# A shared expert's gate and up products moved next to the output projection, and its down product moved ahead of the routed experts

## Chip, cores and metric

The kernel runs on one core of a Trainium2 chip. The metric is the device time of one execution in microseconds, the median of several runs.

## What is computed

Two transformer blocks on 256 tokens of width 1024. The change lies in the second half of the first block, a mixture of 64 routed experts and one shared expert:

```python
x = x + g1 * (jnp.concatenate([y_fox, y_rwkv], axis=-1) @ w_out[l])
h = rms_norm(x, norm2_g[l]) * (1 + sc2) + sh2
x = x + g2 * moe_ffn(h, router_w[l], router_bias[l], exp_w_gate[l], exp_w_up[l], exp_w_down[l],
                     sh_w_gate[l], sh_w_up[l], sh_w_down[l])
# moe_ffn: each token takes 6 of 64 experts, with weights from the sigmoid scores
routed = routed_experts(hf, idx, wts.astype(h.dtype), w_gate, w_up, w_down)
shared = swiglu(hf, sw_gate, sw_up, sw_down)       # (silu(x @ wg) * (x @ wu)) @ wd, inner width 256
```

The norm multiplies each token by one factor r (from the mean square of its 1024 values) and each feature by a gain; then a shift per feature is added. So a product of h with a weight W is r times the product of (gain x) with W, plus the product of the shift with W, which is the same for all tokens.

## The kernel before

All activations are kept transposed, features on the 128 partitions and the 256 tokens (T) along the free axis, as 8 chunks of 128 features (NK). Matmul weights come through a ring of 1 MB buffers: `weights` takes the next buffer in turn and issues the load on SyncE's queue (SP), in program order; a load waits until its buffer's last user is done. The ring is put together in `phase_a`: 3 buffers (RING), 2 more (RINGX) and 7 more (RINGY) that take the place of earlier tiles when the mixers of the first block are finished. The kernel is written against a framework that tracks tiles, puts in all waits and fixes the order of the instructions of each engine when the program is built: earlier lines of the program go first where several are ready by its model, so a later line can be drawn forward into a pause.

Around the change the program runs like this.

- `phase_a` ends with `w_out(1)`, the second half of the output projection. It yields once for each of the 8 chunks d. Each step splits weights in two parts (ACT copies the high part `wh`, GpSimd, called POOL, subtracts the low part `wl`), runs 12 matmuls in PSUM, and DVE adds the residual into `xT[:, d]` (x1). Then `score(d)` multiplies the chunk with the router's weights and squares it (`ssum`, `rsq`).
- After the last chunk `router` forms the norm's factor y per token (`rms2`, `rsqrt`), the scores `lg`, and `rs2`, the factor laid out along the free axis, by a matmul with the diagonal `rdg`.
- `phase_b` calls `route` (a chain of small DVE operations: top groups, top 6, prefix counts by five small matmuls `ps<-rmb,rbef`), then forms the normalised input h2 (shown as `h`) in 8 chunks with DVE, ACT and POOL. `choose(0)` builds the selection matrix P of the first group and its weights (`rtab`, `ws`).
- h2 is transposed on PE (L1194) and split in a high part `hh` (ACT) and a low part `hl` (DVE).
- `shared` is a generator: its first step is the gate product `mm<-h,w` and Silu, before the loop; its second step, the up product, comes after group 0, its third, the down product `acc<-sT,w`, after group 1. h2 lies in one of the two buffers of the tag "xg" until up is done.
- The loop runs over 16 groups of 4 experts. `experts` gathers tokens (`ps<-P,hh` and `ps<-P,hl`, 32 matmuls in four PSUM tiles), evicts them to xg (L1469, DVE and ACT in turn), then for 8 weight units of gate/up and 4 of down multiplies 32 columns per expert (`mm<-w,xg`, `mm<-second,xg`, `mm<-w,hT`, `mm<-second,hT`); "second" is a copy of a unit's part for a second expert (L1484). The results are split (`yh` on ACT, `yl` on DVE) and scattered into four accumulators in PSUM (`acc<-PT,yh`, `acc<-PT,yl`). All 16 groups and the shared expert add into the same accumulators, and the first of them all clears them with `start`.

A product of plain f32 operands, as those of the shared expert, shows as two matmul instructions. All helpers have one line each: matmuls L318, tensor_tensor L325, tensor_scalar L328, scalar_tensor_tensor L331, activations L337, the ring's loads L293.

Of the kernel before, what the change touches and what calls it, by code (L numbers as in the profile page):

```python
# [25 lines left out]
NEG = -1e30  # L26
RING = 3
RINGX = 2
RINGY = 7
NF = 7  # L30
NE = 8
NG = 3
# [233 lines left out]
class Prog:  # L266
# [242 lines left out]
    def phase_a(self):  # L509
        nc = self.nc  # L510
        ctx = ExitStack()
        with ctx:
# [204 lines left out]
            self.xT = late.tile([128, NK, T], F32, name="xT")  # L717
            self.more("ringX", RINGX)
            self.late = ExitStack()
            score = self.router(self.pool("router", ctx=self.late, side="right"))  # L720
            self.more("ringY", RINGY, self.late)
            if self.dbg and "catT" in self.dbg:
                for i in range(4):
                    nc.sync.dma_start(self.dbg["catT"][:, 2 * i:2 * i + 2, :], cat[i])
            for d in w_out(1):
                self.stt(self.xT[:, d, :], self.o[d // 2][:, d % 2, :], self.mod[:, 16 + d:17 + d], x0[d // 2][:, d % 2, :],
                         OP.mult, OP.add)
                score(d)
            self.show("x1T", self.xT)

    def rwkv_prepare(self, big, low, proj, hf):
# [427 lines left out]
    def phase_b(self):  # L1159
        nc = self.nc  # L1160
        ctx = ExitStack()
        with ctx:
            self.psum, self.banks = self.pool("psumB", space=PSUM, ctx=ctx), {"mm": 2, "ps": 2}
            self.pacc = self.pool("pacc", space=PSUM, bufs=1, ctx=ctx)
            self.wk, self.nsq = self.pool("wkB", bufs=2, ctx=ctx), 2
            bb = self.pool("bigB", bufs=1, ctx=ctx)
            self.copied = [None, None]
            R = self.route(bb)

            rs, gs = self.rs2, self.gs2  # L1170

            def normed():
                h2 = self.wk.tile([128, NK, T], F32, tag="xg", name="h2")
                for k in range(NK):
                    self.stt(h2[:, k, :], self.xT[:, k, :], gs[:, k:k + 1], rs, OP.mult, OP.mult)
                    self.act(h2[:, k, :], h2[:, k, :], AF.Identity, bias=self.mod[:, 24 + k:25 + k])
                return h2
            h2 = self.wk.tile([128, NK, T], F32, tag="xg", name="h2")
            for k in range(NK):
                if k % 2:  # L1180
                    self.act(h2[:, k, :], self.xT[:, k, :], AF.Identity, scale=gs[:, k:k + 1])
                    self.tt(h2[:, k, :], h2[:, k, :], rs, OP.mult, nc.gpsimd)
                else:
                    self.stt(h2[:, k, :], self.xT[:, k, :], gs[:, k:k + 1], rs, OP.mult, OP.mult)
                self.act(h2[:, k, :], h2[:, k, :], AF.Identity, bias=self.mod[:, 24 + k:25 + k])
            self.show("h2T", h2)
            first = self.choose(0, R, bb)

            hh, hl = (bb.tile([128, 2, D], F32R, name=n) for n in ("hh", "hl"))
            for b in range(2):  # L1190
                for q in range(2):
                    ps = self.ps("mm")
                    for i in range(4):
                        nc.tensor.transpose(ps[:, 128 * i:128 * i + 128], h2[:, 4 * q + i, 128 * b:128 * b + 128],  # L1194
                                            self.ident)
                    o = slice(512 * q, 512 * q + 512)
                    nc.scalar.copy(hh[:, b, o], ps)
                    self.tt(hl[:, b, o], ps, hh[:, b, o].bitcast(F32), OP.subtract)
            acc = [self.pacc.tile([128, 2, T], F32, tag=f"acc{i}", name=f"acc{i}") for i in range(4)]
            shared = self.shared(h2, acc)  # L1200
            next(shared)
            for g in range(16):
                self.experts(g, R, first if g == 0 else self.choose(g, R, bb), hh, hl, acc)
                if g == 0:
                    self.unplaced(R, bb)
                next(shared, None)
            self.leftovers(R, normed, acc, bb)
            self.fewer(RINGY)
            for d in range(8):
                self.stt(self.xT[:, d, :], acc[d // 2][:, d % 2, :], self.mod[:, 40 + d:41 + d], self.xT[:, d, :],  # L1210
                         OP.mult, OP.add)
# [15 lines left out]
    def router(self, rt):  # L1227

        nc, rw, br = self.nc, self.rw, self.br
        self.lg = rt.tile([128, 2, 64], F32, name="lg")  # L1230
        self.act(self.lg[:, 0, 0:1], br[:, 0:1], AF.Sigmoid)
        self.rs2 = rt.tile([128, T], F32, name="rs2")
        s = rt.tile([128, T], F32, name="ssum")
        pl = self.ps()
        pm = self.ps()

        def score(k):
            for b in range(2):
                self.mm(pl[:, 64 * b:64 * b + 64], self.xT[:, k, 128 * b:128 * b + 128], rw[:, k, :], start=k == 0 and b == 0,
                        stop=k == NK - 1)  # L1240
            sq = s if k == 0 else rt.tile([128, T], F32, tag="rsq", name="rsq")
            self.act(sq, self.xT[:, k, :], AF.Square)
            if 0 < k < NK - 1:
                self.tt(s, s, sq, OP.add)
            if k < NK - 1:
                return
            for i, t in enumerate((s, sq)):
                for b in range(2):
                    self.mm(pm[:, b:b + 1], t[:, 128 * b:128 * b + 128], self.ones[:, 0:1], start=i == 0 and b == 0, stop=i == 1)
            x = rt.tile([128, 2], F32, name="rms2")  # L1250
            self.ts(x, pm[:, 0:2], 1.0 / D, EPS, OP.mult, OP.add)
            y = self.rsqrt(x)
            for b in range(2):
                self.stt(self.lg[:, b], pl[:, 64 * b:64 * b + 64], y[:, b:b + 1], br, OP.mult, OP.add)
            self.act(self.lg, self.lg, AF.Sigmoid)

            dg = rt.tile([128, T], F32, tag="rsq", name="rdg").rearrange("p (b t) -> p b t", b=2)
            for b in range(2):
                self.ts(dg[:, b], self.ident, y[:, b:b + 1], None, OP.mult)
                self.mm(pm[:, T + 128 * b:T + 128 * b + 128], self.ones, dg[:, b])  # L1260
            nc.scalar.copy(self.rs2, pm[:, T:])
        return score

    def shared(self, h2, acc):

        sT = self.wk.tile([128, 2, T], F32, tag="sq", name="sT", bufs=self.nsq)
        sg = self.wk.tile([128, 2, T], F32, tag="sq", name="sgs", bufs=self.nsq)
        for u in range(2):
            w = self.weights(self.a["sh_gu"][u]).rearrange("p (k n) -> p k n", k=NK)
            ps = self.ps("mm")  # L1270
            for c in range(2):
                o = ps[:, T * c:T * c + T]
                for k in range(NK):
                    self.mm(o, w[:, k, 128 * c:128 * c + 128], h2[:, k, :], start=k == 0, stop=k == NK - 1)
            for c in range(2):
                o = ps[:, T * c:T * c + T]
                if u == 0:
                    self.act(sg[:, c, :], o, AF.Silu)
                else:
                    self.tt(sT[:, c, :], sg[:, c, :], o, OP.mult)  # L1280
            yield
        w = self.weights(self.a["sh_d"], 2048).rearrange("p (f n) -> p f n", n=D)
        for d in range(8):
            for f in range(2):
                self.mm(acc[d // 2][:, d % 2, :], w[:, f, 128 * d:128 * d + 128], sT[:, f, :], start=False, stop=False)
        yield

    def route(self, bb):

# [162 lines left out]
    def experts(self, g, R, slots, hh, hl, acc):  # L1452
# [6 lines left out]
        for q in range(4):  # L1459
            ps = self.ps()  # L1460
            for i in range(2):
                d = 2 * q + i
                n = 0
                for b in range(2):
                    for part in (hh, hl):
                        self.mm(ps[:, T * i:T * i + T], part[:, b, 128 * d:128 * d + 128],
                                P[:, b].rearrange("p r s -> p (r s)"), start=n == 0, stop=n == 3)
                        n += 1
            (nc.scalar.copy if q % 2 else nc.vector.tensor_copy)(  # L1469
                xg[:, 2 * q:2 * q + 2, :].rearrange("p k t -> p (k t)"), ps)  # L1470
        eng = [nc.vector, nc.scalar, nc.vector, nc.scalar]
        reg = []
        for q in range(4):
# [32 lines left out]
        for n in range(2):  # L1506
# [7 lines left out]
            for r in range(2):  # L1514
# [5 lines left out]
                for i in range(4):  # L1520
                    d = 4 * n + i
                    for y in (yh, yl):
                        self.mm(acc[d // 2][:, d % 2, :], y[:, 128 * i:128 * i + 128], PT[:, r],
                                start=g == 0 and r == 0 and d % 2 == 0 and y is yh, stop=False)

    def leftovers(self, R, normed, acc, bb):

# [726 lines left out]
```

## Time and profile before

| | us |
|---|---|
| median of 3 runs | 1398.86 (1393.77 to 1401.87) |
| profiled execution | 1392.92 |
| its span, first to last instruction | 1390.9 |
| PE busy in the span | 1274.5 (92%) |
| DVE, ACT, POOL busy | 784.1, 656.0, 359.6 |

Engines: PE is TensorE's matmul row, PEld its weight loads, DVE VectorE, ACT ScalarE, POOL GpSimd, SP SyncE. A matmul's row is longer than the distance to the next one, since they overlap; for costs the distance of starts is read. The busy time of an engine is an average over stages with different limits, so the views below are taken stage by stage: the output projection is at 337 to 359 us, the expert loop at 384 to 900.

### The profile page before, as it was taken

Reading aid. Unit: us, or ns where it says so; the run is one execution under the profiler, and the core shown is the slowest. Engines: PE = TensorE matmul, PEld = TensorE weight load, DVE = VectorE, ACT = ScalarE, POOL = GpSimd, SP = SyncE. Lnnn points to the kernel's source line nnn. Section 1 sums busy time; section 2 is a strip of 40 time slices with the busy share of each in tenths; the row PEclk is TensorE's granted clock in tenths of the full one; section 3 lists DMA queues with packets and bytes.
Section 4 is the critical chain, followed back from the end, with each engine's and each line's share of the span. In section 5 each row is a group of like instructions: output and inputs, shape, how many; then the busy total and the mean of one; then the engine's idle time right before and its main releaser. Section 6 shows DMA issues by size and latency. Waiting matters only on the chain. (4 is left out here: it accounts for less than half of the span.)

```text
span 1390.9 us, 27073 instructions
## 1 busy us (share of the span) xinstructions
PE 1274.5 (92%) x10141; PEld 912.3 (66%) x10141; DVE 784.1 (56%) x2021; ACT 656.0 (47%) x1309; POOL 359.6 (26%) x310
## 2 busy tenths in 40 slices
PE   5888899999799999999999999979899877999996
PEld 4666777778645544444444444458788867999996
DVE  4679835555754355545555554468735457544444
ACT  2531323234364455555555555555444445455552
POOL 0133541103200000000000000044345731166662
PEclk9988999899799999999999999988899988999998
DMA  9443555124588899999999999742122433245530
GB/s 373 162 151 138 196 213 191 61 77 162 232 331 333 335 392 388 395 393 400 391 382 387 393 406 394 282 176 98 62 79 87 143 117 121 85 176 185 181 134 31
DMA packets 47080, 321.04 MB, mean 231 GB/s; under 512 B 5216, under 2 KB 5856, under 8 KB 9184
## 3 DMA queue, kind: packets, MB, share of 16 engines
q1 hardware_dynamic: 45072, 316.17, 58.3%
q10 hardware_dynamic: 1872, 3.08, 0.7%
q8 instruction: 82, 1.34, 0.4%
q14 instruction: 54, 0.44, 0.1%
HBM read 318.19 MB, written 1.05 MB: 230 GB/s over the span
## 5 line engine op out<-in xcount | busy, mean ns | idle before, releaser
L325 POOL TENSOR_TENSOR wl<-w,wh 128x512 fp32r<-128x512 f32 x221 | 290.4, 1331 | 373.1 <-ACT wh L310 247.9
L1484 ACT COPY second<-w 128x512 f32 x384 | 218.3, 619 | 103.9 <-PE mm L318 78.2
L318 PE MATMUL mm<-xh,wh 128*128 128x256 f32 (+1 forms) x768 | 230.5, 300 | 14.8 <-DMA w<-in_w_dram 4.7
L318 PE MATMUL mm<-xh,wl 128*128 128x256 f32 (+1 forms) x768 | 229.9, 300 | 4.0 <-POOL wl L325 3.4
L318 PE MATMUL mm<-xl,wh 128*128 128x256 f32 (+1 forms) x768 | 227.5, 296 | 0.2 <-DVE xl L331 0.2
L1484 DVE COPY second<-w 128x512 f32 x384 | 146.5, 427 | 103.0 <-PE mm L318 93.6
L310 ACT CAST wh<-w 128x512 fp32r<-128x512 f32 x196 | 119.6, 619 | 156.5 <-PE mm L318 117.8
L318 PEld LDWEIGHTS mm<-xh,wh 128*128 128x128 f32 (+1 forms) x768 | 155.6, 203 | 23.2 <-ACT xh L337 4.9
L318 PEld LDWEIGHTS mm<-xh,wl 128*128 128x128 f32 (+1 forms) x768 | 154.7, 202 | 9.6 <-POOL wl L325 4.8
L318 PEld LDWEIGHTS mm<-xl,wh 128*128 128x128 f32 (+1 forms) x768 | 155.2, 202 | 4.6 <-issue 2.1
L328 POOL TENSOR_SCALAR PT<-consts,ws 128x256 fp32r<-128x256 f32 x32 | 30.9, 978 | 474.3 <-DVE ws L1444 462.0
L318 PE MATMUL mm<-w,xg 128*32 128x512 f32 x1024 | 133.9, 594 | 0.0
L318 PE MATMUL mm<-second,xg 128*32 128x512 f32 x1024 | 133.5, 592 | 0.0
L318 PEld LDWEIGHTS mm<-second,xg 128*32 128x32 f32 x1024 | 34.3, 110 | 75.6 <-issue 68.0
L325 DVE TENSOR_TENSOR yl<-mm,yh 128x512 fp32r<-128x512 f32 x64 | 43.7, 689 | 62.1 <-ACT yh L1518 62.1
L318 PEld LDWEIGHTS mm<-w,xg 128*32 128x32 f32 x1024 | 32.0, 110 | 68.8 <-issue 63.1
L318 PE MATMUL mm<-second,hT 128*32 128x512 f32 x512 | 75.7, 594 | 0.0
L318 PE MATMUL mm<-w,hT 128*32 128x512 f32 x512 | 73.3, 602 | 2.5 <-ACT hT L1504 2.5
L318 PE MATMUL ps<-P,hh 128*128 128x256 f32 x256 | 67.6, 293 | 0.7 <-DVE xg L1469 0.7
L318 PE MATMUL ps<-P,hl 128*128 128x256 f32 x256 | 65.9, 287 | 0.0
L1518 ACT CAST yh<-mm 128x512 fp32r<-128x512 f32 x64 | 37.5, 585 | 52.2 <-PE mm L318 51.5
L318 PE MATMUL acc<-PT,yh 128*128 128x256 f32 x256 | 60.8, 287 | 0.3
(628 smaller groups left out, 2511.8 us busy)
## 6 DMA issues: line engine op xcount, KB each, us to landing
w<-in_exp_dram SPq DMA_DIRECT2D x192, 1024.0 KB, 9.4
w<-in_ada_dram SPq DMA_DIRECT2D x24, 1024.0 KB, 5.0
w<-in_ffi_dram SPq DMA_DIRECT2D x22, 1024.0 KB, 4.9
w<-in_w_dram SPq DMA_DIRECT2D x14, 1024.0 KB, 4.8
w<-in_w_in_dram SPq DMA_DIRECT2D x12, 1024.0 KB, 4.8
w<-in_ffo_dram SPq DMA_DIRECT2D x11, 1024.0 KB, 4.7
w<-in_w_out_dram SPq DMA_DIRECT2D x4, 1024.0 KB, 4.9
w<-in_mixout_dram SPq DMA_DIRECT2D x4, 1024.0 KB, 4.9
```

The costliest lines, as they stand in the source:

```text
L310: self.nc.scalar.copy(h, x)
L318: return self.nc.tensor.matmul(o, l, r, start=start, stop=stop, skip_group_check=True).ins
L325: (eng or self.nc.vector).tensor_tensor(out=o, in0=x, in1=y, op=op)
L328: (eng or self.nc.vector).tensor_scalar(out=o, in0=x, scalar1=s1, scalar2=s2, op0=op0, op1=op1)
L1484: c = (nc.scalar.copy if q % 2 else nc.vector.tensor_copy)(s[:, q:q + 1, :], w[:, bass.ds(reg[q], 1), :])
L1518: nc.scalar.copy(yh, ps)
```

## The change

- `gate_up` replaces the first two steps of `shared`. Ahead of the projection's second half it allocates `xg` (8 chunks of 256 columns and one more column), lets POOL copy the shift into that last column, and issues both loads of the shared expert. In each step d of the projection DVE writes gain times x1 into chunk d, without the norm's factor and without the shift. After the last step 64 matmul instructions of 257 columns form gate and up in four PSUM tiles; the last column is the shift's product. DVE copies that column (4 times), multiplies the rest by `rs2` (4 times) and, for up, adds and multiplies in one operation (2 times); ACT does Silu with the column as bias.
- The normalised h2 before the loop is gone. The transposes read `xg`; y, kept in `y2`, is put in where they are evicted: ACT's copy becomes an activation with a scale, DVE's subtraction a scalar_tensor_tensor.
- As the gathered rows now lack the shift, it is added in `experts` where gathers are evicted: on DVE an addition in place of a copy, on ACT two activations of 256 with a bias in place of a copy of 512.
- The down product stands ahead of the loop (`shared_down`), and clears the accumulators.
- RINGY is 6 instead of 7; `ssum` lies in another pool.

```diff
-RINGY = 7
+RINGY = 6
@@ phase_a
+            gu = self.gate_up()
             for d in w_out(1):
                 self.stt(self.xT[:, d, :], ...)
                 score(d)
+                self.ts(self.xg[:, d, :T], self.xT[:, d, :], self.gs2[:, d:d + 1], None, OP.mult)
+            gu()
@@ phase_b
-            h2 = self.wk.tile([128, NK, T], F32, tag="xg", name="h2")
-            for k in range(NK):
...
                     for i in range(4):
-                        nc.tensor.transpose(ps[:, 128 * i:128 * i + 128], h2[:, 4 * q + i, 128 * b:128 * b + 128],
+                        nc.tensor.transpose(ps[:, 128 * i:128 * i + 128], self.xg[:, 4 * q + i, 128 * b:128 * b + 128],
                                             self.ident)
-                    nc.scalar.copy(hh[:, b, o], ps)
-                    self.tt(hl[:, b, o], ps, hh[:, b, o].bitcast(F32), OP.subtract)
+                    self.act(hh[:, b, o], ps, AF.Identity, scale=y)
+                    self.stt(hl[:, b, o], ps, y, hh[:, b, o].bitcast(F32), OP.mult, OP.subtract)
-            shared = self.shared(h2, acc)
-            next(shared)
+            self.shared_down(acc)
             for g in range(16):
                 self.experts(g, R, first if g == 0 else self.choose(g, R, bb), hh, hl, acc)
-                next(shared, None)
+    def gate_up(self):
+        nc, rt = self.nc, self.rt
+        self.xg = xg = rt.tile([128, NK, T + 1], F32, name="xgain")
+        nc.gpsimd.tensor_copy(xg[:, :, T], self.mod[:, 24:32])
+        ws = [self.weights(self.a["sh_gu"][u]).rearrange("p (k n) -> p k n", k=NK) for u in range(2)]
+        def f():
+            self.sT = sT = rt.tile([128, 2, T], F32, name="sT")
+            sg = self.wk.tile([128, 2, T], F32, tag="sq", name="sgs", bufs=self.nsq)
+            for u in range(2):
+                for c in range(2):
+                    ps = self.ps(("po", "pt", "mm", "mm")[2 * u + c])
+                    for k in range(NK):
+                        self.mm(ps[:, :T + 1], ws[u][:, k, 128 * c:128 * c + 128], xg[:, k, :T + 1], start=k == 0, stop=k == NK - 1)
+                    t = (sT if u else sg)[:, c, :]
+                    b = self.wk.tile([128, 8], F32, tag="nx", name="gub", bufs=3)[:, :1]
+                    nc.vector.tensor_copy(b, ps[:, T:T + 1])
+                    self.tt(t, ps[:, :T], self.rs2, OP.mult)
+                    if u == 0:
+                        self.act(t, t, AF.Silu, bias=b)
+                    else:
+                        self.stt(t, t, b, sg[:, c, :], OP.add, OP.mult)
+        return f
@@ experts
-            (nc.scalar.copy if q % 2 else nc.vector.tensor_copy)(
-                xg[:, 2 * q:2 * q + 2, :].rearrange("p k t -> p (k t)"), ps)
+            p, sh = ps.rearrange("p (k t) -> p k t", k=2), self.mod[:, 24 + 2 * q:26 + 2 * q]
+            if q % 2:
+                for i in range(2):
+                    self.act(xg[:, 2 * q + i, :], p[:, i], AF.Identity, bias=sh[:, i:i + 1])
+            else:
+                self.tt(xg[:, 2 * q:2 * q + 2, :], p, sh[:, :, None].to_broadcast([128, 2, T]), OP.add)
```

## Rows read from the trace of the kernel before

**Rows 1.** Busy us by stretch: length, PE, PEld, DVE, ACT, POOL, clock, DMA.

```profile
337.00:359.00 22.00, 20.51 (x164) 19.45 (x162) 9.67 (x17) 9.99 (x20) 11.60 (x9) 0.99 1.00 418
359.00:384.00 25.00, 16.21 (x70) 12.71 (x71) 20.59 (x113) 8.98 (x20) 4.85 (x6) 0.66 0.32 132
...
630.00:662.00 32.00, 31.34 (x265) 14.61 (x264) 17.03 (x48) 18.19 (x34) 2.00 (x2) 1.00 0.99 396
```

**Rows 2.** Waits, 384 to 900 us: total us, times, longest; all engines, then SP's queue.

```profile
PEld mm L318 <- DMA w<-in_exp_dram: 4.7, 16, 0.3
...
SPq L293 <- PE mm L318: 322.3, 174, 28.9
```

**Rows 3.** PE's timeline in the loop: start us, length, instruction, how many merged.

```profile
389.22 1.06 PE L318 MATMUL mm<-w,xg 128*32 128x512 f32 x8
...
418.72 7.07 PE L318 MATMUL mm<-h,w 128*128 128x256 f32 x32
425.43 0.47 PE L318 MATMUL ps<-P,hh 128*128 128x256 f32 x1
...
429.34 1.06 PE L318 MATMUL mm<-w,xg 128*32 128x512 f32 x8
...
459.08 6.63 PE L318 MATMUL acc<-sT,w 128*128 128x256 f32 x30
...
468.72 1.07 PE L318 MATMUL mm<-w,xg 128*32 128x512 f32 x8
...
501.08 1.07 PE L318 MATMUL mm<-w,xg 128*32 128x512 f32 x8
...
629.96 1.06 PE L318 MATMUL mm<-w,xg 128*32 128x512 f32 x8
...
662.06 1.06 PE L318 MATMUL mm<-w,xg 128*32 128x512 f32 x8
```

**Rows 4.** PE ahead of the loop: timeline, then groups of 359 to 386 us.

```profile
358.59 0.28 PE L318 MATMUL fx<-yh,wl 128*128 128x256 f32 x1
...
384.18 0.47 PE L318 MATMUL ps<-P,hh 128*128 128x256 f32 x1
...
L318 PE MATMUL mm<-h,w 128*128 128x256 f32 x32 | 9.0, 443 | 1.0 <-issue 1.0
L1194 PE MATMUL mm<-consts,h 128*128 128x128 f32 x16 | 4.7, 438 | 5.1 <-ACT h L337 3.8 <-DVE hl L325 1.2
```

**Rows 5.** DVE, 359 to 384 us: groups (busy us, mean ns), then the timeline.

```profile
L331 DVE SCALAR_TENSOR_TENSOR h<-xT,gs,rs 128x256 f32<-128x256 f32 x4 | 2.8, 691 | 0.0
L325 DVE TENSOR_TENSOR hl<-mm,hh 128x512 fp32r<-128x512 f32 x4 | 2.7, 682 | 0.0
...
L331 DVE SCALAR_TENSOR_TENSOR xT<-fx,mod,x 128x256 f32<-128x256 f32 x1 | 0.5, 484 | 0.9 <-PE fx L318 0.9
...
379.32 0.68 DVE L325 TENSOR_TENSOR hl<-mm,hh 128x512 fp32r<-128x512 f32 x1
```

**Rows 6.** SP's timeline: loads issued from 330 us on.

```profile
335.34 0.33 SPq L293 DMA_DIRECT2D w<-in_sh_gu_dram  x1
337.04 47.86 SPq L293 DMA_DIRECT2D w<-in_exp_dram  x12
```

**Rows 7.** ACT and DVE evictions: groups of 500 to 890 us; timeline at 367 us.

```profile
L1469 ACT COPY xg<-ps 128x512 f32<-128x512 f32 x25 | 14.6, 585 | 36.5 <-PE ps L318 36.5
...
L1469 DVE COPY xg<-ps 128x512 f32<-128x512 f32 x25 | 17.3, 692 | 15.8 <-PE ps L318 15.8
...
366.98 1.31 ACT L337 ACTIVATE h<-h,mod 128x256 f32<-128x256 f32 x3 [0.18 <-POOL h L325]
```

**Rows 8.** Busy us in steps of 2 us, columns as in the first group.

```profile
358.00:360.00 2.00, 1.76 (x17) 1.68 (x15) 0.48 (x1) 0.42 (x1) 0.00 (x0) 1.00 1.02 422
...
362.00:364.00 2.00, 1.04 (x4) 0.93 (x4) 1.92 (x14) 0.82 (x2) 0.00 (x0) 0.50 1.04 434
...
378.00:380.00 2.00, 2.00 (x9) 1.70 (x8) 2.00 (x10) 0.00 (x0) 0.00 (x0) 0.86 0.00 0
```

More of the change, by code (lines that the diff above doesn't have):

```diff
@@ L719, in phase_a @@
             self.late = ExitStack()
-            score = self.router(self.pool("router", ctx=self.late, side="right"))
+            self.rt = self.pool("router", ctx=self.late, side="right")
+            score = self.router(self.rt)
             self.more("ringY", RINGY, self.late)
@@ L1177, in normed @@
                 return h2
-            h2 = self.wk.tile([128, NK, T], F32, tag="xg", name="h2")
-            for k in range(NK):
[L1180 to L1186, printed above, removed]
             first = self.choose(0, R, bb)
@@ L1190, in phase_b @@
             for b in range(2):
+                y = self.y2[:, b:b + 1]
                 for q in range(2):
@@ L1232, in router @@
         self.rs2 = rt.tile([128, T], F32, name="rs2")
-        s = rt.tile([128, T], F32, name="ssum")
+        s = self.wk.tile([128, T], F32, tag="hk", name="ssum")
         pl = self.ps()
@@ L1252, in score @@
             y = self.rsqrt(x)
+            self.y2 = rt.tile([128, 2], F32, name="y2")
             for b in range(2):
@@ L1255, in score @@
             self.act(self.lg, self.lg, AF.Sigmoid)
+            nc.vector.tensor_copy(self.y2, y)
             dg = rt.tile([128, T], F32, tag="rsq", name="rdg").rearrange("p (b t) -> p b t", b=2)
@@ L1262, in router, with shared_down @@
         return score
[L1264 to L1281, printed above, removed]
+    def gate_up(self):
[20 more added lines that the diff above has]
+        return f
+    def shared_down(self, acc):
         w = self.weights(self.a["sh_d"], 2048).rearrange("p (f n) -> p f n", n=D)
@@ L1284, in shared @@
             for f in range(2):
-                self.mm(acc[d // 2][:, d % 2, :], w[:, f, 128 * d:128 * d + 128], sT[:, f, :], start=False, stop=False)
-        yield
+                self.mm(acc[d // 2][:, d % 2, :], w[:, f, 128 * d:128 * d + 128], self.sT[:, f, :], start=d % 2 == 0 and f == 0,
+                        stop=False)
     def route(self, bb):
@@ L1523, in experts @@
                         self.mm(acc[d // 2][:, d % 2, :], y[:, 128 * i:128 * i + 128], PT[:, r],
-                                start=g == 0 and r == 0 and d % 2 == 0 and y is yh, stop=False)
+                                start=False, stop=False)
     def leftovers(self, R, normed, acc, bb):
```

## The prediction, made before the changed kernel was built

> **What bounds the kernel now.** I looked first for the engine that never rests. A table of stretches [rows 1] shows TensorE (PE) busy for 31.34 us of the 32 us from 630, in the middle of the expert loop, at the full granted clock (1.00), and for 20.51 of 22 us in the output projection. Between them stands a hole, 359 to 384 us: PE is busy 16.21 of 25 us at a mean granted clock of 0.66, while VectorE (DVE) is busy 20.59 us. The DMA's share of 0.99 in the loop could mean that weights are late, so the list of waits comes next [rows 2]: PE's weight loads waited 4.7 us in all for an expert's weights in the whole loop, and the DMA queue waited 322.3 us for PE to give buffers back. The loop is bound by PE, the weights follow it. So a PE instruction taken out of the loop is worth its full time, and one put into the hole before it costs only what doesn't fit there.
>
> The timeline of PE gives the loop's beat [rows 3]. The first gate/up product of a group starts at 389.22, 429.34, 468.72, 501.08 and, far in, 629.96 and 662.06: group 0 takes 40.12 us, group 1 takes 39.38, group 2 takes 32.36, a late one 32.10. Groups 0 and 1 are longer because the shared expert rides in them: its up product (32 instructions from 418.72) and its down product (30 of 32 from 459.08), each with PE to itself for some 6.7 us.
>
> **The change, part by part.**
>
> *Out of the loop.* Up leaves group 0, down leaves group 1. From 418.72 to the next gather at 425.43 is 6.71 us for 32 instructions, 0.21 us each [rows 3]. With them goes a second loss: the normalised input of the shared expert holds one of the two "xg" buffers until up is done, so group 1's gathers run after 425.43 in one piece, not in the pauses of group 0. I therefore let both groups fall to group 2's length and not only by the products: 40.12 + 39.38 - 2 x 32.36 = **14.8 us**. The bare products (2 x 6.7 = 13.4) are the lower bound, the late groups' length (2 x 32.1) the upper, 15.3.
>
> *Into the hole.* The last projection matmul starts at 358.59, the first gather at 384.18 [rows 4]; 25.6 us have to hold gate, up and down now. In instructions: gate and up 64 x 0.2165 = 13.9 us (0.21 to 0.22 each at the full clock, the one added column in 257 included), down 32 x 0.2165 = 6.9, 16 transposes at half of the 4.7 us that they took at half clock = 2.4, and the router's 25 small ones (8 for the norm, 4 of the last score, 4 for `rs2`, 5 prefix counts, 4 for `rtab`) at half of an up instruction, 2.6, an estimate. Sum 25.8 us: they just fit, if PE keeps the full clock and never stands still. Today the same stretch holds only gate (32 instructions, 9.0 us because much of it ran at half clock) and the same transposes [rows 4]. Standstill that I expect: after up, PE has only transposes (whose evictions by ScalarE, ACT, and DVE alternate on two banks) until DVE has finished the product sT for down. Today's four hl subtractions take 2.7 us in all [rows 5]; I put it at **+1.5 us**. The bounds: below, gate matmuls that fill the 1.5 us in which PE rests during the projection [rows 1], hence -1.5; above, 32 down instructions at half clock, 6.9 us more, hence +8.4.
>
> *DVE's chain to the first group.* It mustn't grow, or the first gather waits for it and not for PE. Out go four normalising operations, 2.8 us, 0.69 each against 0.48 for an operation of the same shape a moment earlier [rows 5]; GpSimd's four beside them go too. In come four evictions with the norm's factor and two products, each priced as the 0.48 us xT product of 256 out of PSUM (2.9 us), and four copies of one column, under 0.2 each: 3.5 us. hl stays one DVE operation of its shape. Net +0.7 us (0 to 1), off the chain as long as it is done while the route waits for PE. That wait is new: the five small matmuls of the route's prefix sum stand behind 64 gate/up instructions, and DVE's later route and the first selection behind them. Today the last hl is done at 380.0 and PE gathers only at 384.18 [rows 4, 5], so 4 us of this are covered; beyond that each us is one on the first gather. Eight gain operations (256 elements, at most 0.48 us) go into the projection loop; DVE is idle over half of it [rows 1] (9.67 of 22 us busy), so 0. The one small copy on GpSimd stands ahead of the weight splits of the projection in its queue; the space it writes has to be free, and the loads into the buffers beside it issue at 335.34 and 337.04 [rows 6]; 0, or 1.7 us (the distance of the two) if it holds up a split.
>
> *Weights.* Both shared loads and the down load now go ahead of the experts', and the ring has 11 buffers for 12. SP issues one shared load at 335.34 and 11 expert loads from 337.04 on; the twelfth ends that row at 337.04 + 47.86 - 0.33 = 384.57, and at 378 the DMA moves nothing [rows 6, 8]: the ring is full long before the loop. After: three shared and 8 expert loads by then, and three more as gate, up and down give their buffers back. The queue then waits for PE and not PE for it [rows 2], and a buffer less of lead is a twelfth of a group, 2.7 us: 0, or at most those 4.7 us again.
>
> *In every group.* The shift is added where gathers are evicted: on DVE a copy of 0.69 us [rows 7] becomes an addition, and hl's subtraction of the same shape took 0.68 [rows 5], so 0; on ACT a copy of 0.585 us becomes two halves with a bias, each like the 0.50 us Identity of this trace, pitch (1.31 - 0.50) / 2 = 0.40 [rows 7], about 0.9 together. That is 0.3 us more, twice a group, on an engine busy 18.2 of 32 us [rows 1]. I take 0, since 32 x 0.3 = 9.6 us at worst is a rival. By the Trainium skill, "ScalarE: Activation LUTs", What ACT_TABLE_LOAD costs, an ACTIVATE with a bias pointer takes 280 ns + 0.833 ns per element (493 for 256) and one with immediates 186 ns + the same (612 for 512); the rows agree (500 and 585), and the sum would be the same.
>
> **Sum.** -14.8 + 1.5 = -13.3 us; all other terms are 0 within their bounds. The profiled execution took 1392.92 us (span 1390.9 and 2.0 around it), so 1379.6 for such a one; it lies 5.9 us under the median of the three runs, 1398.86, from which I forecast **1385.6 us**. What follows the loop only starts earlier.
>
> **The rivals.**
> - *The hole is too small.* Idle time lets the clock fall and down runs at 0.43 us an instruction: -13.3 + 6.9 = -6.4, **1392.5**. For: the granted clock was 1.00 at 358 to 360, with PE busy 1.76 of 2 us, 0.50 at 362 to 364, with PE busy for half of it, and 0.86 on average at 378 to 380, where gate ran without a pause [rows 8]. Against: 64 matmuls in one piece follow the projection now, so PE has no reason to rest there.
> - *Slower.* The same, but for all of it: gate and up start only after a rest, because a projection step or a score in front of them in PE's order waits for DVE; then 64 + 32 instructions run at half clock: 20.8 us more, -13.3 + 20.8 = +7.5, **1406.4**. It decides from 62 of the 96 instructions on (62 x 0.2165 = 13.4). By the Trainium skill, "TensorE: Matmul & The Clock Gate", Part 1, the slow clock is the default and sustained activity lifts it; rows 8 agree with both directions. By that rule alone, without a rest ahead of gate, this case falls away, since the new order fills the hole.
> - *ACT's two halves.* If each of the 32 longer evictions holds up PE by its 0.3 us, 9.6 us are given back: -13.3 + 9.6 = -3.7, **1395.2**. For: two ps banks, and PE needs the eviction to gather on. Against: in the loop it is ACT that waits for PE's gathers, not PE for ACT.
> - *Doesn't do what it says:* down, ready late, is ordered behind work of group 0 and stays in the loop: -13.3 + 6.7 = -6.6, **1392.3**; the time is that of the first rival, the trace differs.
>
> **How the numbers follow.** The likeliest case gets 0.58 (its own range 1381 to 1391: start -1.5 to +5, late-group length, and the 3 us by which medians of such runs move); the hole too small 0.14, ACT 0.10, down still in the loop 0.07, slower 0.06; 0.05 for a larger gain (late groups' beat from the start and a first gather 1.5 us earlier, -15.3 - 1.5 = -16.8, **1382** or less). The range 1378 to 1396 leaves out the slow case, part of ACT's and what no case foresees, some 0.2 together. A measurement of this kernel tells about 0.5%, 7 us, from no change. Faster by more: 0.56 of the likeliest, the larger gain and half of the first and the last rival, 0.72. Within: the other halves and ACT's case, 0.21. Slower by more: half of the slow case and something unseen, 0.07.
>
> **What would show it.** Groups 0 and 1 near 32.4 us on PE's timeline; a first gather at 384 to 387; gate/up as 64 matmuls at 0.22 us right behind the projection with the granted clock at 1.00 up to 374; down complete ahead of the first gather; PE's wait for weights unchanged; later groups at 32.1. Wrong if the first gather comes after 393, if the clock stands at 0.50 while gate runs, or if the late groups grow by over 0.3 us each.

## The result and the profile after

The changed kernel takes 1382.22 us (median of 6 runs, 1372.02 to 1386.41) beside 1393.34 us for the kernel before in the same comparison (1392.51 to 1401.87). The ratio is 0.9894, 95% interval 0.9868 to 0.9919: 11 to 18 us faster; the two medians alone differ by 11.1. A second comparison gave 1379.87 us and 0.9896 (0.9838 to 0.9954).

Stretches of the changed kernel's first profile, with the columns of [rows 1]: the end of the projection, the hole behind it, the middle of the expert loop. This profile runs some 7 us early from 280 us on, so the stretches are shifted.

```profile
330.00:352.00 22.00, 20.25 (x163) 19.40 (x162) 12.58 (x23) 9.88 (x20) 12.16 (x10) 0.98 0.98 405
352.00:377.00 25.00, 24.49 (x136) 21.40 (x135) 21.54 (x122) 5.93 (x10) 1.62 (x2) 1.00 0.50 187
623.00:655.00 32.00, 31.40 (x264) 14.63 (x264) 16.95 (x49) 18.62 (x38) 2.00 (x2) 1.00 0.98 392
```

The middle row is the change. Where PE was busy 16.21 of 25 us at a granted clock of 0.66 [rows 1], it is now busy 24.49 of 25 at 1.00. The loop's row is as before.

PE's timeline in that hole, in the columns of [rows 3]:

```profile
349.23 0.59 PE L318 MATMUL po<-xgain,w 128*128 128x257 f32 x2
...
351.85 0.28 PE L318 MATMUL fx<-yh,wl 128*128 128x256 f32 x1
...
352.33 1.11 PE L318 MATMUL po<-xgain,w 128*128 128x257 f32 x4
353.29 0.55 PE L318 MATMUL ps<-rw,xT 128*128 128x64 f32 x4
...
354.10 2.42 PE L318 MATMUL po<-xgain,w 128*128 128x257 f32 x10
356.35 0.59 PE L318 MATMUL pt<-xgain,w 128*128 128x257 f32 x2
...
357.24 3.21 PE L318 MATMUL pt<-xgain,w 128*128 128x257 f32 x14
360.29 7.12 PE L318 MATMUL mm<-xgain,w 128*128 128x257 f32 x32
367.25 0.31 PE L318 MATMUL ps<-rmb,rbef 128*128 128x64 bf16 x5
367.39 1.07 PE L1190 MATMUL mm<-consts,xgain 128*128 128x128 f32 x8
368.30 0.60 PE L318 MATMUL acc<-sT,w 128*128 128x256 f32 x2
369.41 0.27 PE L318 MATMUL ps<-rtab,P 128*128 128x10 f32 x1 [0.51 <-DVE P L325]
369.54 0.68 PE L318 MATMUL acc<-sT,w 128*128 128x256 f32 x2
...
371.03 1.04 PE L1190 MATMUL mm<-consts,xgain 128*128 128x128 f32 x8
371.90 2.76 PE L318 MATMUL acc<-sT,w 128*128 128x256 f32 x12
...
374.64 2.84 PE L318 MATMUL acc<-sT,w 128*128 128x256 f32 x12
377.12 0.47 PE L318 MATMUL ps<-P,hh 128*128 128x256 f32 x1
```

Gate begins inside the projection (two instructions at 349.23) and goes on right behind it. Gate and up run to 367.25, then come the prefix counts, the transposes and down, and the first gather follows at 377.12. From the last projection matmul (351.85) to the first gather it is 25.27 us, where it was 25.59 [rows 4]. In all of it PE rests once for something: 0.51 us, for DVE's P.

The starts of the groups in the loop:

```profile
381.80 1.07 PE L318 MATMUL mm<-w,xg 128*32 128x512 f32 x8
...
414.97 0.64 PE L318 MATMUL mm<-w,xg 128*32 128x512 f32 x4
...
447.58 0.64 PE L318 MATMUL mm<-w,xg 128*32 128x512 f32 x4
...
480.16 1.07 PE L318 MATMUL mm<-w,xg 128*32 128x512 f32 x8
...
511.86 0.64 PE L318 MATMUL mm<-w,xg 128*32 128x512 f32 x4
...
640.15 1.06 PE L318 MATMUL mm<-w,xg 128*32 128x512 f32 x8
...
672.23 1.06 PE L318 MATMUL mm<-w,xg 128*32 128x512 f32 x8
```

Group 0 takes 33.17 us (40.12 before), group 1 32.61 (39.38 before), group 2 32.58, group 3 31.70, a late one 32.08 [rows 3].

This first profile's span is 1370.3 us, 20.6 less than before. But 6.74 us of that lie ahead of its last projection matmul, and they are there from 280 us on, before anything that the change touches. The second profile of the same kernel says what that is:

```profile
358.74 0.28 PE L318 MATMUL fx<-yh,wl 128*128 128x256 f32 x1
...
384.00 0.47 PE L318 MATMUL ps<-P,hh 128*128 128x256 f32 x1
...
388.67 1.07 PE L318 MATMUL mm<-w,xg 128*32 128x512 f32 x8
```

There the projection ends at 358.74, 0.15 us from the kernel before [rows 4], and the span is 1375.9 us. So the 6.7 us came with that execution and not with the change. Taken against this second profile the account is: hole 25.26 against 25.59, -0.3; first gather to first product 4.67 against 5.04, -0.4; the fifteen groups from first product to last start 482.81 against 497.37, -14.6; the two stretches outside, +0.2. Together -15.0 us (1390.9 to 1375.9).

### The profile page after: what moved, and what is told of

It reads as the page before. It is cut to its first block, busy times and chain, and to the rows that moved or that the text cites. A ratio compares the mean times of both kernels' runs of the same rounds, so it can differ in the third digit from the quotient of the medians.

```text
span 1370.3 us, 27102 instructions
## 1 busy us (share of the span) xinstructions
PE 1263.3 (92%) x10141; PEld 903.6 (66%) x10141; DVE 783.8 (57%) x2034; ACT 659.1 (48%) x1329; POOL 357.6 (26%) x307
```

## The experiments

**The same kernel once more, and down left in the loop.** The first label is the changed kernel unedited, measured beside the next three. The second moves the down product alone back to where it stood.

```diff
-            self.shared_down(acc)
             for g in range(16):
                 self.experts(g, R, ...)
 ...
+                if g == 1:
+                    self.shared_down(acc)
 ...
```

> The changed kernel once more, to separate what the change does from what its profiled execution happened to be. That one was 1372.02 us, ten under its other runs, and 6.7 us of its lead over the profile of before lie ahead of the last projection matmul (351.85 against 358.59). Theory 'only the loop and the hole are changed': the last projection matmul of a new profile comes at 358 +- 4, the distance from it to the first gather is again 25.3 us, the loop's first sixteen starts span 482.9 us, and the time is 0.985 to 0.992 of before. Rival 'the earlier stage gained too': the last projection matmul comes again at 352 and the time is 0.984 to 0.987.

> Only the down product goes back to its place behind group 1; all else as in the changed kernel. Theory 'the hole is closed by DVE': DVE's last hl ends 0.5 us ahead of the first gather in the changed kernel, so taking 6.9 us of PE work out of the hole brings the first gather forward by 0.5 us at most, group 1 grows from 32.6 to 39.3 us, and the time is 6 to 7 us above the changed kernel's. Rival 'the hole is full of PE work, every instruction in it counts': the first gather comes 6 to 7 us earlier and the total stays within 1 us of the changed kernel's.

The unedited kernel did what the first theory says: last projection matmul at 358.74, first gather 25.26 us behind it, sixteen starts in 482.81 us, 0.9896 of before.

With down back in the loop: 1384.4 us, ratio 0.9917 (0.9884 to 0.9949), 4.5 us more than the changed kernel beside it; the intervals of the two overlap, the traces do not leave it open. Down runs in group 1 again (30 of its 32 instructions from 448.33), which takes 39.53 us, and the fifteen groups take 490.63, 7.8 more. PE's waits between the last projection matmul and the first gather (total us, times, longest), then two stretches there, then DVE's timeline and PE's first gather:

```profile
PE ps L318 <- DVE P L331: 1.5, 1, 1.5
PE ps L318 <- DVE P L325: 0.9, 1, 0.9
PE mm L1190 <- DVE hl L331: 0.5, 1, 0.5
```

```profile
374.00:376.00 2.00, 0.64 (x3) 0.47 (x4) 2.00 (x11) 0.77 (x2) 0.00 (x0) 0.98 0.78 279
...
378.00:380.00 2.00, 0.60 (x3) 0.61 (x4) 2.00 (x9) 0.60 (x1) 0.00 (x0) 0.50 0.00 0
```

```profile
377.95 1.65 DVE L331 SCALAR_TENSOR_TENSOR P<-consts,rc,P 128x128 fp32r<-128x128 f32 x6
...
379.69 0.73 DVE L331 SCALAR_TENSOR_TENSOR hl<-mm,y,hh 128x512 fp32r<-128x512 f32 x1
```

```profile
379.63 0.56 PE L318 MATMUL ps<-P,hh 128*128 128x256 f32 x1
```

The hole has 6.8 us less of PE work (32 instructions at 0.21) but is only 2.9 us shorter, 22.33: PE now waits 2.9 us for DVE, which is busy for all 2 us of both stretches, and part of the rest runs at half clock. The first gather waits for P and not for the last hl: it starts right behind P's last piece (377.95 + 1.65 = 379.60) and ahead of the third and the fourth hl (379.69 and 381.33). That is 22.3 us behind the last projection matmul. So some 22 us is what the chain over DVE to P needs, and down fills room that stood empty. The expected total (6 to 7 us) came out as 6.0 in the trace; that the gather would hardly move was wrong, it came 2.9 us nearer, of which 1.1 was lost again in gathers at half clock (first gather to first product 5.79 against 4.67).

**Gate held back until after a rest.** The shift's column is written only after `rs2` is there, with the same values, so that gate can't begin behind the projection.

```diff
-        nc.gpsimd.tensor_copy(xg[:, :, T], self.mod[:, 24:32])
 ...
+            self.ts(z, self.rs2[:, 0:8], 0.0, None, OP.mult, eng=nc.gpsimd)
+            self.tt(xg[:, :, T], self.mod[:, 24:32], z, OP.add, nc.gpsimd)
```

> The column of the shift is written only after the norm's factor rs2 is there (two operations of eight columns on GpSimd), so that gate and up, unchanged otherwise, begin some 5 us after the last projection matmul and not 0 to 2 us after it. Theory 'the clock of the hole depends on gate following without a rest': PE rests ahead of gate, the granted clock falls to 0.50 there, gate runs its first instructions at 0.43 us, and the first gather comes 6 to 12 us later than in the changed kernel; the loop is as in the changed kernel. Rival 'only the wait itself counts': the clock stays at 1.00 and the first gather comes 4 to 5 us later.

Measured: 1388.79 us, ratio 0.9956 (0.9932 to 0.998), 8.9 us over the changed kernel beside it; in the trace the hole grows by 6.9 us to 32.13 and the loop stays (483.09). Stretches of it, columns of [rows 1], and PE's timeline:

```profile
362.00:364.00 2.00, 0.30 (x1) 0.30 (x2) 1.86 (x12) 0.31 (x1) 0.00 (x0) 0.56 0.98 414
...
366.00:368.00 2.00, 1.97 (x5) 1.60 (x6) 1.79 (x13) 0.64 (x1) 0.00 (x0) 0.50 0.00 0
...
370.00:372.00 2.00, 2.00 (x11) 1.74 (x10) 0.71 (x4) 0.18 (x1) 0.00 (x0) 1.00 0.00 0
```

```profile
366.03 5.22 PE L318 MATMUL po<-xgain,w 128*128 128x257 f32 x16 [1.10 <-POOL xgain L325]
371.09 3.64 PE L318 MATMUL pt<-xgain,w 128*128 128x257 f32 x16
374.57 7.12 PE L318 MATMUL mm<-xgain,w 128*128 128x257 f32 x32
```

After PE had rested for most of 362 to 366 the granted clock stood at its lower level, 0.50, and with gate running it was back at 1.00 from 370. The first 16 instructions took 371.09 - 366.03 = 5.06 us, 0.32 each on average, the next 16 3.48 and the 32 of up 6.96, 0.22 each. Thus the clock itself costs 16 x 0.10 = 1.6 us here and the later start the other 5.3. By the Trainium skill, "TensorE: Matmul & The Clock Gate", Part 1, the slow clock is the default and sustained activity lifts it; these rows agree.

**No shared expert at all.** Gate, up, down and their evictions are left out (the shared expert is missing from the result); their loads, the gain operations and the shift in the gathers stay.

```diff
-            gu()
 ...
-                self.mm(acc[d // 2][:, d % 2, :], w[:, f, 128 * d:128 * d + 128], self.sT[:, f, :], ...)
 ...
```

> Leaves out the shared expert: no gate, up and down matmuls and none of their evictions; its three loads and the gain's eight operations stay. What is saved against the changed kernel is what the shared expert still costs there. Theory 'nearly hidden': DVE's chain loses 3.5 us of evictions and the route's prefix counts no longer wait 3.3 us behind up, while PE rests and its clock falls as in the kernel before; the first gather comes 4 to 7 us earlier and the loop is the same. Rival 'PE work in the hole is paid in full': 20 us earlier.

Measured: 1382.79 us, ratio 0.9897 (0.9839 to 0.9956): not faster than with the shared expert (1379.87 beside it). PE's waits between the last projection matmul and the first gather:

```profile
PE ps L318 <- DVE rtab L325: 5.8, 1, 5.8
PE ps L318 <- DVE rmb L331: 4.0, 1, 4.0
```

Some 20 us of PE work are gone and the hole is only 4.0 us shorter, 21.22; PE waits for the route's chain on DVE instead. Those 4.0 us are then lost behind it. First gather to first product is 0.9 longer, at a granted clock of 0.54 (382 to 388 us). Group 0 takes 36.37 us instead of 33.17, where the same loop was expected. The clock is 1.00 through all of that group (387.91 to 424.28), so these 3.2 us are not the clock's but an order's: eight of the 32 gathers stand behind the group's first two products (388.89 to 390.04), and PE waits 1.9 us for DVE's h where it waited 0.4. In the place where the change puts it, the shared expert therefore costs at most the 4.0 us of the hole, of its 20 us of products; measured against this program without it, it costs nothing.

**What the 1.4 us beside the products were.** This is the kernel before, with a buffer of its own for h2 and a weight buffer fewer.

```diff
-RINGY = 7
+RINGY = 6
 ...
-            h2 = self.wk.tile([128, NK, T], F32, tag="xg", name="h2")
+            h2 = bb.tile([128, NK, T], F32, name="h2own")
```

> The kernel before with one edit: the normalised h2 gets a buffer of its own and leaves the xg buffers alone (one weight buffer fewer, 11, makes room). Gate, up and down stay where they were. My sum for the loop, 14.8 us, held 13.4 us of products and 1.4 us for the xg buffer that h2 keeps until up is done. If the buffer carries that part, group 0 falls from 40.12 us by 1.0 us (0.7 to 1.4) and group 1 stays at 39.4. The rival: the products are all of it, group 0 stays within 0.3 us of 40.12, and the 1 us more that group 0 takes in the changed kernel's loop too (33.17 against 32.1) has another cause. Total either way within 3 us of the kernel before.

Measured: 1391.18 us, ratio 0.9957 (0.9924 to 0.9989), 2 to 11 us less than the kernel before, where at most 3 were expected. The starts of groups 0, 1 and 2:

```profile
385.90 0.63 PE L318 MATMUL mm<-w,xg 128*32 128x512 f32 x3
...
426.02 0.64 PE L318 MATMUL mm<-w,xg 128*32 128x512 f32 x4
...
465.43 0.64 PE L318 MATMUL mm<-w,xg 128*32 128x512 f32 x4
```

Group 0 takes 40.12 us and group 1 39.41, as before the edit. The buffer cost nothing; my reason for that part falls. What the loop gained is the products (group 0 by 6.95, group 1 by 6.77) and small shifts in groups that do the same work: group 2 +0.22, group 3 -0.66, group 4 -0.27. The edit also shortened the hole by 1.7 us and the way from gather to product by 0.8; the first products of gate stand elsewhere in PE's order there, and I did not follow it further. These 2.5 us are what the trace shows of the shorter time.

**One weight buffer fewer.** `RINGY` is 5 in place of 6 in the changed kernel.

> The changed kernel with 10 weight buffers in place of 11. My term for the lost buffer was 0: the queue waits for TensorE and not TensorE for it. Then one buffer fewer changes nothing either: PE's wait for an expert's weights stays at 4 to 5 us, the late groups at 32.07 us, the time within 2 us of the changed kernel. The rival, that the lead had become short with 11 buffers, expects waits of 1 us and more per group, 16 us and more in all.

Measured: 1382.8 us, ratio 0.9893 (0.9863 to 0.9923), late groups 32.07. PE's waits for an expert's weights in the whole loop, first the changed kernel, then with one buffer fewer:

```profile
PEld mm L318 <- DMA w<-in_exp_dram: 4.2, 14, 0.3
```

```profile
PEld mm L318 <- DMA w<-in_exp_dram: 2.7, 9, 0.3
```

Before it was 4.7 [rows 2]. Neither the buffer that the change takes away nor another one is felt. Group 3, 31.69 us in the changed kernel, is 32.08 in this one, with the same 264 PE instructions in another order: 0.4 of the 0.66 us that this group gained hang on the order that the framework picks and not on the change itself.

**ACT's eviction in four pieces.**

```diff
-                    self.act(xg[:, 2 * q + i, :], p[:, i], AF.Identity, bias=sh[:, i:i + 1])
+                    for b in range(2):
+                        o = slice(128 * b, 128 * b + 128)
+                        self.act(xg[:, 2 * q + i, o], p[:, i, o], AF.Identity, bias=sh[:, i:i + 1])
```

> The changed kernel with ScalarE's eviction of the gathers cut into four pieces of 128 columns in place of two of 256, with the same bias. It doubles the suspected cost of the two halves. My term was 0, since ScalarE waits for the gathers and not TensorE for ScalarE: then the late groups stay at 32.07 us (within 0.1) and the time within 2 us of the changed kernel. The rival, in which each longer eviction holds up TensorE, expects some 0.35 us more on each of 32 evictions, 0.7 us on each group and 11 us in all.

Measured: 1388.73 us, ratio 0.9929 (0.99 to 0.9957), some 6 us over the kernel with one buffer fewer beside it, so neither forecast was met. The groups of ACT's evictions in the late loop (count, busy us, mean ns), the changed kernel's two pieces and then the four, and the start of two late groups with four pieces:

```profile
L337 ACT ACTIVATE xg<-ps,mod 128x256 f32<-128x256 f32 x41 | 18.5, 475 | 30.8 <-PE ps L318 30.8
```

```profile
L337 ACT ACTIVATE xg<-ps,mod 128x128 f32<-128x128 f32 x80 | 25.2, 370 | 29.8 <-PE ps L318 29.8
```

```profile
592.08 0.64 PE L318 MATMUL mm<-w,xg 128*32 128x512 f32 x4
...
624.21 0.64 PE L318 MATMUL mm<-w,xg 128*32 128x512 f32 x4
```

The late groups take 32.13 us: twice the pieces cost 0.05 us a group, not 0.7, and ACT still waits for PE. That settles the rival for the later groups. Groups 0 to 3 are 34.14, 33.49, 33.49 and 33.77, 4.8 us more in all, and first gather to first product is 1.2 us less. In these four groups and in no later one PE's order is another: eight gathers stand behind the group's first two products, where the changed kernel has all of them ahead. From the first product to the next gather it is 0.98 us in each of the four. It is the same 0.98 us (387.91 to 388.89) in group 0 of the run without the shared expert, which has this order with ACT's two pieces. So what these groups lose comes with the order and not with the four pieces: the edit changed the plan.

**DVE's work in the hole moved and put in another order.** The transposes and their evictions go by halves of the features first, ACT copies the four shift columns, POOL writes constants of the route.

```diff
-            for b in range(2):
-                y = self.y2[:, b:b + 1]
-                for q in range(2):
+            for q in range(2):
+                for b in range(2):
+                    y = self.y2[:, b:b + 1]
 ...
-                    nc.vector.tensor_copy(b, ps[:, T:T + 1])
+                    nc.scalar.copy(b, ps[:, T:T + 1])
 ...
-        nc.vector.memset(tab.bitcast(F32), 0.0)
+        nc.gpsimd.memset(tab.bitcast(F32), 0.0)
 ...
```

> The changed kernel with VectorE's work in the hole made shorter by about 1.5 us and nothing else: the halves of hl that the first gathers need are formed first (the last 0.74 us subtraction is then wanted only by later gathers), ScalarE copies the four shift columns, GpSimd writes the constants of the route. If VectorE's chain sets the first gather, as the runs without the shared expert and with down in the loop let me think, the distance from the last projection matmul to the first gather falls from 25.3 us by 1 to 2 us. If TensorE's 25 us of work set it, as I summed it, it stays within 0.4 us. The total moves by less than 2 us.

Measured: 1379.88 us, ratio 0.9862 (0.9828 to 0.9897); the hole is 25.39 us, 0.1 more than in the changed kernel, and the fifteen groups take 482.90. The last hl on DVE and the first gather on PE, then P on DVE in the changed kernel's first profile:

```profile
385.83 0.74 DVE L331 SCALAR_TENSOR_TENSOR hl<-mm,y,hh 128x512 fp32r<-128x512 f32 x1
```

```profile
387.13 0.47 PE L318 MATMUL ps<-P,hh 128*128 128x256 f32 x1
```

```profile
372.51 1.65 DVE L331 SCALAR_TENSOR_TENSOR P<-consts,rc,P 128x128 fp32r<-128x128 f32 x6
```

In this order that last hl belongs to the later gathers, and still the first gather comes no earlier. But the chain itself did not get shorter: DVE's busy time in the hole fell by 0.5 us only (21.54 to 21.07, not 1.5), DVE then waited 1.4 us for ACT's copy of a shift column behind up, and P was ready 22.4 us and the last hl 24.8 us behind the last projection matmul, both as in the changed kernel. So this run alone can't tell which of the two sets the first gather. The changed kernel's own trace does: P is ready at 372.51 + 1.65 = 374.16, 3.0 us ahead of the first gather, and PE has no rest from 369.41 up to it. The theory that I had made from the two runs above, that DVE's chain sets the first gather in the changed kernel, falls: PE's own work does, 24.8 us of it and 0.5 of rest, and the chain's 21 to 22 us lie beneath. The time is inside the changed kernel's interval, so this is no better version.

## Why the prediction held, point by point

Predicted were 1385.6 us and a range of 1378 to 1396; 1382.22 was measured. The mechanism was the one named as likeliest; two terms were mis-sized and one reason was wrong. The total says less than the terms, since its start moves too: the forecast began at 1398.86, the median of three runs, where the six runs of this comparison have 1393.34 and 21 later ones 1398.17.

- *Out of the loop, -14.8.* Measured -14.5 and -14.6. But groups 0 and 1 did not come down to 32.36: they took 33.17 and 32.61, which is the products alone (13.7 us). The part that I gave to the xg buffer is not there, as the kernel with h2 in a buffer of its own shows. What filled the sum were shifts of 0.2 to 0.7 us in groups 2 to 4 that no step foresaw, so that the term came out to 0.3 us is luck. The bare products, which I had as the lower bound, would have been the better value for these two groups.
- *Into the hole, +1.5.* Measured -0.3; this term carries most of the miss. Of the 25.8 us summed for PE's work, 24.8 were measured: by the starts above 13.7 for the 62 gate and up instructions behind the projection, 6.8 for down, 1.8 for the transposes and about 2.5 for the small ones. The transposes were priced too high (half of the 4.7 us of their group at half clock, where sixteen at the full clock take 1.8), and two gate instructions found room in the projection, the gain that I had named only as the lower bound. The standstill, put at 1.5 us ahead of down, was 0.51.
- *DVE off the path.* It holds, by another reason than the one given. I had 4 us of cover between the last hl at 380.0 and the first gather at 384.18 [rows 4, 5]; in the changed kernel the last hl ends at 376.6, 0.5 us ahead of the gather, and the four hl take 0.74 us each and not 0.68. But the first gather waits for P, ready 5.8 us ahead of it before (376.70 + 1.66 = 378.36) and 3.0 us now. DVE's busy time in the hole grew by 0.95 us (20.59 to 21.54), where 0.7 was forecast. What covers all this is PE's work: with 6.8 or 20 us less of that, the hole stops at 22.3 and 21.2 us.
- *Eight gain operations and POOL's copy, 0.* DVE's busy time at the end of the projection went from 9.67 [rows 1] to 12.58 us. The gain operations took 0.56 us each on average and not 0.48 at most: five of them 0.34 to 0.36 us, three 0.50, 0.87 and 1.37, all three while POOL was splitting weights. On the same instructions the second profile is 0.11 us early at 340 us and 0.15 late at the last projection matmul, with 0.44 us of gate in between: 0 holds.
- *Weights, 0; ACT's halves and DVE's addition, 0.* PE's wait for weights was 4.2 us, 5.1 in the second profile, and the run with 10 buffers is as fast. ACT's piece took 475 ns where I priced 500, DVE's addition 691 where its copy took 692 [rows 7], and the late groups are 32.06 to 32.09 as before.
- *Not in the sum.* First gather to first product fell by 0.4 us.
- *The rivals.* A hole too small and down at half clock did not come: the clock is 1.00 through all of it. The slower case was made on purpose by holding gate back, and its price was wrong: I let all 96 instructions run at half clock, 20.8 us, while only the first 16 paid, 1.6 us, and the rest of the 6.9 was a later start. Gate, running without a pause, brought the clock back by itself there, so the rival could not have reached the other side in that way; with 6.9 us lost, the trace's -15.0 would still be -8.1. Down left in the loop was made too: 6.0 us in the trace, where 6.7 were priced.

The sum for one execution, -13.3, stands against -15.0 in the second profile.

## What to carry to other kernels

A pause of the busiest engine is worth as much work as lies between that engine's load in it and the chain that keeps it waiting: here the chain over DVE needs 21 to 22 us and PE's other work there 4 to 5, so 20.4 us of a shared expert's products fitted in for some 4 us of length that the hole had anyway. Work put there must be ready before the pause begins, which is what the factored norm bought: gate ran behind the projection without a gap, and held back until after a rest it cost 7 us. To learn which of two nearly equal chains ends a stretch, shorten each by itself, and see in the trace that it did get shorter: 6.8 us less for PE brought the first gather 2.9 us nearer, while the work taken from DVE left its chain as long as it was. And look for the input that is waited for: the last hl lay next to the first gather, but P was what it needed.

## What the runs showed of the hardware

Two executions of the same kernel differ by 6.9 us ahead of the change. Of the stretch from 200 to 240 us the first row is the first profile of the changed kernel, the second is its second profile (columns of [rows 1]):

```profile
200.00:240.00 40.00, 39.30 (x508) 29.36 (x508) 24.48 (x70) 16.00 (x42) 8.42 (x9) 1.00 0.58 198
```

```profile
200.00:240.00 40.00, 39.30 (x422) 28.97 (x421) 19.46 (x58) 14.30 (x39) 7.25 (x7) 0.86 0.48 166
```

PE is busy the same 39.30 of 40 us in both, at a granted clock of 1.00 and of 0.86. The order of its instructions is the same, and the 507 that take 40.0 us in the first profile (200.12 to 240.12) take 44.55 in the second (200.92 to 245.47). The kernel before has 0.86 there too. So part of the 6 to 19 us by which runs of one kernel differ here is the clock of an early stage, and why it differs with the same work the traces do not say.

Short rests can cost more than their length. With down taken out of the hole, PE waited 0.9, 0.5 and 1.5 us, and the granted clock was 0.50 from 376 to 382 us, into the first gathers, which took 1.1 us longer to the first product than in the changed kernel. The single rest of 0.51 us in the changed kernel's hole left the clock at 1.00.
